# First modulation columns by TensorE, eight MLP pairs begun, folds on GpSimd: four edits to a two-layer hybrid encoder trunk

## The chip, the cores and the metric

One core of a Trainium2 chip runs the whole program in one launch. The metric is the device time of one execution in microseconds (us). The kernel before took 2339.54 us, the median of three runs (2332.86 to 2339.99). TensorE appears as PE, VectorE as DVE, ScalarE as ACT, GpSimd as POOL and SyncE, which issues the transfers, as SP.

## The reference, cut to what matters

The input is x (1, 1024, 1024) in f32, a conditioning vector c of 1024 and the weights. There are two layers. Layer 0 mixes by an mLSTM, layer 1 by multi-head latent attention. Every sub-layer is normalised before and after, and shifted, scaled and gated by rows made from c:

```python
c_act = jax.nn.silu(c)
for layer in range(DEPTH):
    sh1, sc1, g1, sh2, sc2, g2 = jnp.split(c_act @ mod_w[layer] + mod_b[layer], 6, axis=-1)
    h = modulate(rms_norm(x, norm_g[layer, 0]), sh1, sc1)
    ...
    x = x + g1[:, None, :] * rms_norm(y, norm_g[layer, 1])
    h = modulate(rms_norm(x, norm_g[layer, 2]), sh2, sc2)
    y = sq_relu_mlp(h, ffn_w1[layer], ffn_w2[layer])
    x = x + g2[:, None, :] * rms_norm(y, norm_g[layer, 3])
```

`sq_relu_mlp` is `square(relu(h @ w1)) @ w2` with w1 of 1024 x 4096. Each of the rows sh1 to g2 is a product of c_act (1024) with 1024 columns of mod_w.

## The kernel before, in words

Every large product is made of three TensorE products: both operands are cut into a high and a low part (`whi` and `wlo` of a weight, `hTh` and `hTl` or `uh` and `ul` of an activation), and `mm3` (L155 to L157) multiplies high by high, low by high and high by low. The high part is a cast on ACT, the low part a subtraction on DVE (L106, L504, L550, L754, L442), so each piece of weight passes ACT, then DVE, then PE.

The program is written in one order, and a scheduler with a timeline of its own decides for each engine in which order its instructions stand. Each engine then works through its own list in that order and waits at an instruction whose inputs are not there.

**Start.** `layer_a` normalises the first four token blocks, turns them by TensorE transposes (`turned`, L982) and multiplies them with the value weights, 344 columns at a time, for k = 0 to 7. The turned block k is shifted and scaled, for which the columns sh1 and sc1 of block k are needed. `slab(k)` loads 1024 x 256 of mod_w in two pieces, `mod_sum(k)` (L963 to L970) multiplies and adds the eight 128-row parts on DVE into two accumulators and adds these on POOL, and `mod_col` (L976) sums over partitions by two matmuls with a column of ones.

**Modulation rows.** The other rows come from `layer_mod`, through `gemv`: eight steps on DVE, each with 512 KB of mod_w (L263 for the first, L265 for seven), then eight transposes on PE (`column`, L183) with a DVE reduction. These are generators: `next(mods)` emits one step. In layer 0 two steps go with each value product (the loops below `mods`, L1045), and rows that aren't done there follow with the rest of the mixer. Three rows of layer 1 and a fourth alone (`extra`, L1732) are emitted in the up product of the MLP, one step in every third product.

**Turn to the MLP.** `mixer_out` makes the output projection block by block (n = 0 to 7), adds it to x, and calls `h_norm` (L489), which normalises a block for the MLP by itself. Blocks are turned in pairs: even and odd ones. `odd_sums` (L468, its sums are L476 to L479) makes combinations of the odd blocks with the even ones. `mlp_begin` (L625) does products 1 and 2 of the first BEGUN = 6 of 16 weight pairs, which need only the even blocks and the pair's first weights (`w_first`, L495), while the last blocks are normalised and turned, and makes the high and low parts of the combined blocks (`odd_high`, `odd_low`, L438 and L442).

**MLP.** The MLP's two products use a scheme with seven products in place of eight. In the up product (`up_product`) each pair p runs products 1, 2, 6, 7, 5, 4, 3, and the sums go to DVE (L680, L711 to L714). Weight pairs (`w_pair`) have four sums and differences on POOL (L557, L558, L570, L577), with casts and cuts on ACT (L546) and DVE (L550). In the down product (`mlp`) four token groups j accumulate y in SBUF (DVE L760 adds a PSUM bank to y), and after the last group of pairs but one, seven additions of 128 x 512 fold the accumulators (L816 to L825, all on DVE). These folds stand between DVE's splits of the next u (L754) and the adds L760 that PE waits for to get PSUM banks back; the final products follow.

Of the kernel before, what the change touches and what calls it, by code (L numbers as in the profile page):

```python
# [14 lines left out]
ALU = mybir.AluOpType  # L15
# [50 lines left out]
class Trunk:  # L66
# [356 lines left out]
    BEGUN = 6  # L423
# [65 lines left out]
    def h_norm(self, t):  # L489
        x = self.mix[5].pop(t)  # L490
        h = self.U("h")[:, :D]
        self.S.activation(h, x, AF.Copy, scale=self.rms(x, D, h))
        self.mix[6][t] = h
# [134 lines left out]
    def mlp_begin(self, l, odd):  # L628
# [8 lines left out]

        up(0, 2, 4)
        self.odd_high(0, "S2", "S3")
        self.h_norm(NT - 1)  # L640
        up(1, 3)
        self.w_step()
# [5 lines left out]
        up(3, 4, 5)  # L648
        self.odd_sums(2)
        self.w_step()  # L650
        up(4, 5)
        self.odd_high(2, "S2", "S3", "S1", "A22", "S4")
        self.odd_low(2, "S2", "S3")
        for _ in range(2):
            self.w_step()
        up(5)
        self.w_step()
        self.odd_low(2, "S1", "A22", "S4")
# [60 lines left out]
    def mlp(self, l, done, extra, last=None):  # L719
# [43 lines left out]
        for p in range(NP):  # L763
            for o, s in enumerate((1, 2, 6, 7, 5, 4, 3)):
# [6 lines left out]
                if n % 3 == 0:  # L771
                    next(extra, None)
# [13 lines left out]
        for it in range(items - 4):  # L786
# [28 lines left out]
            if g == ng - 2:  # L815
                for dst, src in (  # L816
                    (c16[:, hi], c16[:, lo]),
                    (c23[:, lo], c16[:, lo]),
                    (c47[:, hi], c16[:, hi]),
                    (c47[:, lo], c47[:, hi]),  # L820
                    (c47[:, hi], fives[j]),
                    (c16[:, hi], fives[j]),
                    (c23[:, hi], c16[:, hi]),
                ):
                    V.tensor_tensor(out=dst, in0=dst, in1=src, op=ALU.add)  # L825
                acc[j] = c23, c47
# [60 lines left out]
    def layer_a(self):  # L887
# [85 lines left out]
        def mod_col(k, acc, ps):  # L973

            for s in range(2):
                PE.matmul(ps[:, s : s + 1], acc[:, s * P : (s + 1) * P], self.ones[:, 0:1], start=True, stop=True)  # L976
# [5 lines left out]
        def turned(k):  # L982

            ps = self.MM()
            mod_col(k, sums.pop(k), ps[:, 512:])
# [16 lines left out]
        mod_sum(0)  # L1002
        for k in range(1, 4):
            slab(k)
        for k in range(1, 4):
            mod_sum(k)
# [29 lines left out]
        for tb in range(4):  # L1036
# [12 lines left out]
            + [lambda j=j: self.layer_mod(1, j) for j in (0, 1)]  # L1049
            for s in mod()  # L1050
        )
        for tb in range(4, NT):
            values(tb, proj_piece(w, tb))
            for _ in range(2):
                next(mods, None)
# [72 lines left out]
    def mixer_out(self, n, y):  # L1128
# [13 lines left out]
        if n == 5:  # L1142
            self.odd_sums(0)
        for t in {2: (0, 1), 3: (2,), 4: (3, 4), 5: (6,), 6: (5,)}.get(n, ()):
            self.h_norm(t)
# [582 lines left out]
    def run(self):  # L1728
# [3 lines left out]
        extra = [(s for j in js for s in self.layer_mod(1, j)) for js in ((2, 4, 3), (5,))]  # L1732
# [99 lines left out]
```

## Time and profile before

| | us |
|---|---|
| median of 3 runs | 2339.54 |
| lowest and highest run | 2332.86 and 2339.99 |
| the profiled execution | 2336.43 |
| its span, first to last instruction | 2334.7 |
| PE busy in it | 2208.0 (95%) |
| DVE, ACT, POOL busy | 1752.7, 1007.7, 480.7 |
| mean granted TensorE clock | 0.988 |

The profile is of one execution. In a row of the timeline stand the start, the duration, the engine, the line of the kernel, the operation, the tiles and shapes, and in brackets the idle time of that engine before the row and what ended it. A busy PE is not PE at its peak, since matmuls overlap; a pace is better read from the distance between starts.

### The profile page before, as it was taken

To read this page: it belongs to the slowest core of one execution; us is meant where nothing else is said; L and a number is where in the kernel's file an instruction comes from. 1 tells how busy PE (TensorE), PEld (TensorE's weight loads), DVE (VectorE), ACT (ScalarE), POOL (GpSimd) and SP (SyncE) were. 2 spreads that over 40 slices of the span, in tenths; PEclk is the share of its full clock that TensorE was granted. 3 is DMA by queue.
4 is the path that set the end of the run, shared out by engine and by line. 5 is a ranking of instruction groups with operands and counts; after the bars stand their busy time and mean duration, and the time that the engine had idled before them with its cause. 6 is when DMAs were issued, how large, how long until landed. Compare 5 with 4: busy or idle time off the path is not lost. (4 is left out here: it accounts for less than half of the span.)

```text
span 2334.7 us, 29139 instructions
## 1 busy us (share of the span) xinstructions
PE 2208.0 (95%) x10730; PEld 1833.8 (79%) x10730; DVE 1752.7 (75%) x2848; ACT 1007.7 (43%) x1637; POOL 480.7 (21%) x324
## 2 busy tenths in 40 slices
PE   5799999988999999999999999999889999999997
PEld 4798888866777777777798988987667888777776
DVE  6684676577888858788998676655777777588888
ACT  4421474563443464233344545544634444633321
POOL 1000110003433334231121000000034334333300
PEclk9999999999999999999999999999999999999999
DMA  9495343233665555454321000122346445544452
GB/s 272 142 322 201 100 73 99 91 109 127 221 226 189 190 180 160 119 167 146 102 88 44 17 17 15 46 73 81 109 156 220 152 149 189 172 131 140 142 174 99
DMA packets 304102, 318.09 MB, mean 136 GB/s; under 512 B 15976, under 2 KB 256216, under 8 KB 303960
## 3 DMA queue, kind: packets, MB, share of 16 engines
q1 hardware_dynamic: 303960, 316.23, 43.2%
q8 instruction: 84, 1.38, 0.2%
q14 instruction: 58, 0.48, 0.1%
HBM read 243.75 MB, written 72.43 MB: 135 GB/s over the span
## 5 line engine op out<-in xcount | busy, mean ns | idle before, releaser
L155 PE MATMUL mm<-whi,uh 128*128 128x512 f32 x688 | 273.1, 397 | 12.6 <-DVE y L760 10.7
L157 PE MATMUL mm<-whi,ul 128*128 128x512 f32 x688 | 271.2, 394 | 1.2 <-DVE ul L754 1.2
L156 PE MATMUL mm<-wlo,uh 128*128 128x512 f32 x688 | 271.1, 394 | 0.0
L577 POOL TENSOR_TENSOR tt<-raw,tt 128x512 f32<-128x512 f32 x60 | 118.0, 1967 | 668.7 <-DVE wlo L550 586.9
L760 DVE TENSOR_TENSOR y<-y,mm 128x1024 f32<-128x1024 f32 (+1 forms) x161 | 193.2, 1206 | 49.6 <-PE mm L157 49.4
L155 PE MATMUL sm<-hSh,whi 128*128 128x512 f32 x512 | 204.2, 399 | 11.3 <-DVE x L680 6.7
L157 PE MATMUL sm<-hSh,wlo 128*128 128x512 f32 x512 | 202.0, 396 | 2.2 <-DVE wlo L550 2.2
L156 PE MATMUL sm<-hSl,whi 128*128 128x512 f32 x512 | 202.5, 396 | 0.0
L550 DVE TENSOR_TENSOR wlo<-raw,whi 128x1024 fp32r<-128x1024 f32 x108 | 162.8, 1507 | 19.8 <-ACT whi L546 18.7
L754 DVE TENSOR_TENSOR ul<-u,uh 128x896 fp32r<-128x896 f32 (+1 forms) x120 | 151.0, 1289 | 32.0 <-ACT uh L748 24.4
L155 PEld LDWEIGHTS mm<-whi,uh 128*128 128x128 f32 x688 | 129.2, 188 | 49.2 <-DVE y L760 17.3
L680 DVE TENSOR_TENSOR x<-x,sm 128x512 f32<-128x512 f32 x192 | 127.8, 681 | 45.3 <-PE sm L157 41.9
L557 POOL TENSOR_TENSOR tt<-raw,raw 128x512 f32<-128x512 f32 x32 | 56.3, 1760 | 489.6 <-DVE hSl L442 461.5
L157 PEld LDWEIGHTS mm<-whi,ul 128*128 128x128 f32 x688 | 129.2, 188 | 32.4 <-DVE ul L754 2.1
L156 PEld LDWEIGHTS mm<-wlo,uh 128*128 128x128 f32 x688 | 129.2, 188 | 29.3
L748 ACT CAST uh<-u 128x896 fp32r<-128x896 f32 (+1 forms) x120 | 107.9, 945 | 84.8 <-PE mm L157 66.9
L265 DVE SCALAR_TENSOR_TENSOR acc<-modw,cact,acc 128x1024 f32<-128x1024 f32 x84 | 112.5, 1339 | 35.8 <-DMA modw<-in_mod_w_dram 29.1
L683 ACT ACTIVATE x<-x 128x1024 f32<-128x1024 f32 x64 | 67.7, 1058 | 155.2 <-DVE x L680 155.2
L582 ACT CAST w<-tt 128x512 fp32r<-128x512 f32 x60 | 37.2, 620 | 213.6 <-POOL tt L577 210.5
L155 PEld LDWEIGHTS sm<-hSh,whi 128*128 128x128 f32 x512 | 96.8, 189 | 37.9 <-DVE x L680 8.2
L546 ACT CAST whi<-raw 128x1024 fp32r<-128x1024 f32 x108 | 112.9, 1045 | 23.9 <-DVE wlo L550 10.2
L546 ACT CAST whi<-tt 128x1024 fp32r<-128x1024 f32 x60 | 62.9, 1048 | 136.9 <-issue 62.2
(404 smaller groups left out, 5991.7 us busy)
## 6 DMA issues: line engine op xcount, KB each, us to landing
raw<-in_ffn_w_dram SPq DMA_DIRECT2D x140, 512.0 KB
u<-us SPq DMA_DIRECT2D x112, 448.0 KB
us<-x SPq DMA_DIRECT2D x92, 512.0 KB
modw<-in_mod_w_dram SPq DMA_DIRECT2D x80, 512.0 KB
x<-xn SPq DMA_DIRECT2D x24, 512.0 KB
x<-x SPq DMA_DIRECT2D x24, 512.0 KB
x<-in_x_dram SPq DMA_DIRECT2D x16, 512.0 KB
slab<-in_mod_w_dram SPq DMA_DIRECT2D x32, 256.0 KB
```

The source lines that it names most:

```text
L155: mm(out, a[0], b[0], start=start, stop=False)
L156: mm(out, a[0], b[1], start=False, stop=False)
L157: mm(out, a[1], b[0], start=False, stop=stop)
L265: self.V.scalar_tensor_tensor(out=acc, in0=t, scalar=self.cact[:, k : k + 1], in1=acc, op0=ALU.mult, op1=ALU.add)
L546: S.copy(x[0], u)
L550: V.tensor_tensor(out=x[1], in0=u, in1=x[0].bitcast(F32), op=ALU.subtract)
L577: G.tensor_tensor(out=t1, in0=b21, in1=t2, op=ALU.subtract)
L680: V.tensor_tensor(out=dst, in0=src, in1=ps, op=ALU.add)
L683: S.activation(u, u, AF.Relu)
L748: S.copy(x[0], u)
L754: V.tensor_tensor(out=x[1], in0=u, in1=x[0].bitcast(F32), op=ALU.subtract)
L760: V.tensor_tensor(out=dst, in0=dst, in1=ps, op=ALU.add)
```

## The change

1. **First columns.** For k = 0 and 1 `mod_col` no longer takes a sum by DVE and POOL: 16 matmuls on PE (8 parts, 2 columns), with the slab as weights and a column of c_act as the moving operand, accumulate the two columns in PSUM. k = 2 to 7 stay as they were.
2. **Modulation rows.** The loop over the values of blocks 4 to 7 emits no steps of `mods` any more, so every row comes later; the row (1, 1) leaves `mods` and goes into `extra`, whose steps are emitted in two of five up products, in place of one of three.
3. **Begin.** BEGUN goes from 6 to 8. `h_norm` takes groups of blocks that share one reciprocal root. `odd_sums(0)` moves from block n = 5 of the output projection to the start of `mlp_begin`, whose steps are put in another order.
4. **Folds.** Four of the seven fold additions of each token group go to POOL.

```diff
-    BEGUN = 6
+    BEGUN = 8
...
-    def h_norm(self, t):
-        x = self.mix[5].pop(t)
-        h = self.U("h")[:, :D]
-        self.S.activation(h, x, AF.Copy, scale=self.rms(x, D, h))
-        self.mix[6][t] = h
+    def h_norm(self, *ts):
+        xs = [self.mix[5].pop(t) for t in ts]
+        ssq = self.W("ssqs", [P, 4])
+        hs = [self.U("h")[:, :D] for _ in ts]
+        for i, (x, h) in enumerate(zip(xs, hs)):
+            self.S.activation(h, x, AF.Square, accum_out=ssq[:, i : i + 1])
+        r = self.rsqrt(ssq[:, : len(ts)], len(ts), 1.0 / D)
+        for i, (t, x, h) in enumerate(zip(ts, xs, hs)):
+            self.S.activation(h, x, AF.Copy, scale=r[:, i : i + 1])
+            self.mix[6][t] = h
...
+        self.odd_sums(0)
         up(0, 2, 4)
+        self.h_norm(NT - 1)
         self.odd_high(0, "S2", "S3")
-        self.h_norm(NT - 1)
         up(1, 3)
-        self.w_step()
         self.odd_high(0, "S1", "A22", "S4")
         self.odd_low(0, "S2", "S3")
         up(2, 3, 5, 4)
         self.odd_turn(2, [odd.pop(5), odd.pop(7)])
         self.odd_low(0, "S1", "A22", "S4")
-        up(3, 4, 5)
+        up(3, 4, 5, 6)
         self.odd_sums(2)
+        up(4, 5, 7, 6)
+        self.odd_high(2, "S2", "S3", "S1")
         self.w_step()
-        up(4, 5)
-        self.odd_high(2, "S2", "S3", "S1", "A22", "S4")
+        up(5, 6, 7)
+        self.odd_high(2, "A22", "S4")
         self.odd_low(2, "S2", "S3")
-        for _ in range(2):
-            self.w_step()
-        up(5)
         self.w_step()
-        self.odd_low(2, "S1", "A22", "S4")
+        up(6, 7)
+        self.w_step()
+        self.odd_low(2, "S1")
+        self.w_step()
+        up(7)
+        self.w_step()
+        self.odd_low(2, "A22", "S4")
         self.w_step()
...
-                if n % 3 == 0:
+                if n % 5 in (0, 2):
                     next(extra, None)
...
-                for dst, src in (
-                    (c16[:, hi], c16[:, lo]),
-                    (c23[:, lo], c16[:, lo]),
-                    (c47[:, hi], c16[:, hi]),
-                    (c47[:, lo], c47[:, hi]),
-                    (c47[:, hi], fives[j]),
-                    (c16[:, hi], fives[j]),
-                    (c23[:, hi], c16[:, hi]),
+                for e, dst, src in (
+                    (G, c16[:, hi], c16[:, lo]),
+                    (G, c47[:, hi], c16[:, hi]),
+                    (G, c47[:, lo], c47[:, hi]),
+                    (G, c23[:, lo], c16[:, lo]),
+                    (V, c47[:, hi], fives[j]),
+                    (V, c16[:, hi], fives[j]),
+                    (V, c23[:, hi], c16[:, hi]),
                 ):
-                    V.tensor_tensor(out=dst, in0=dst, in1=src, op=ALU.add)
+                    e.tensor_tensor(out=dst, in0=dst, in1=src, op=ALU.add)
...
         def mod_col(k, acc, ps):
             for s in range(2):
-                PE.matmul(ps[:, s : s + 1], acc[:, s * P : (s + 1) * P], self.ones[:, 0:1], start=True, stop=True)
+                o = slice(s * P, (s + 1) * P)
+                if acc is not None:
+                    PE.matmul(ps[:, s : s + 1], acc[:, o], self.ones[:, 0:1], start=True, stop=True)
+                else:
+                    for i in range(KD):
+                        PE.matmul(ps[:, s : s + 1], slabs[k][i // 4][:, i % 4, o], self.cact[:, i : i + 1], start=i == 0, stop=i == KD - 1)
...
-        mod_sum(0)
         for k in range(1, 4):
             slab(k)
-        for k in range(1, 4):
+        for k in range(2, 4):
             mod_sum(k)
...
-            + [lambda j=j: self.layer_mod(1, j) for j in (0, 1)]
+            + [lambda: self.layer_mod(1, 0)]
             for s in mod()
         )
         for tb in range(4, NT):
             values(tb, proj_piece(w, tb))
-            for _ in range(2):
-                next(mods, None)
...
-        if n == 5:
-            self.odd_sums(0)
-        for t in {2: (0, 1), 3: (2,), 4: (3, 4), 5: (6,), 6: (5,)}.get(n, ()):
-            self.h_norm(t)
+        for ts in {3: ((0, 2),), 4: ((1, 3),), 5: ((4, 6),), 6: ((5,),)}.get(n, ()):
+            self.h_norm(*ts)
...
-        extra = [(s for j in js for s in self.layer_mod(1, j)) for js in ((2, 4, 3), (5,))]
+        extra = [(s for j in js for s in self.layer_mod(1, j)) for js in ((1, 2, 4, 3), (5,))]
```

Three places show what this does to the engines' lists. The names are tiles with a buffer number: `sm` and `mm` are PSUM banks, `acc` a sum of a modulation row, `ident` the matrix for transposes. Lines of the changed kernel are a few higher than those before (L504 becomes L509).

The first place is PE's list among the value products of blocks 4 to 7. Before, the first row's transposes stand here:

```order
L155 MATMUL sm_1012<-whi_552,hTh_785 128x344
L156 MATMUL sm_1012<-wlo_553,hTh_785 128x344
L157 MATMUL sm_1012<-whi_552,hTl_786 128x344
L183 MATMUL sm_1039<-ident,acc_855 128x128 x4
L183 MATMUL sm_1045<-ident,acc_855 128x128 x4
L155 MATMUL sm_1075<-whi_544,hTh_698 128x344
L156 MATMUL sm_1075<-wlo_545,hTh_698 128x344
```

In the changed kernel they stand here, and a transpose of the gates stands 55 rows behind the old place:

```order
L156 MATMUL sm_1192<-wlo_820,hTh_465 128x344
L157 MATMUL sm_1192<-whi_819,hTl_466 128x344
L183 MATMUL sm_1219<-ident,acc_1020 128x128 x4
L183 MATMUL sm_1225<-ident,acc_1020 128x128 x4
L155 MATMUL sm_1231<-whi_807,hTh_215 128x344
L156 MATMUL sm_1231<-wlo_808,hTh_215 128x344
```

The transposes went from row 392 of PE's list to row 536, 144 rows later.

The second place is the start of PE's list. `slab` is a piece of mod_w, `x` a token block. Before:

```order
L976 MATMUL mm_213<-ones,acc_151 128x1 x2
L183 MATMUL mm_213<-ident,x_95 128x128
L183 MATMUL mm_213<-ident,x_97 128x128
L183 MATMUL mm_213<-ident,x_111 128x128
L183 MATMUL mm_213<-ident,x_113 128x128
L976 MATMUL mm_252<-ones,acc_180 128x1 x2
```

After:

```order
L991 MATMUL mm_191<-cact,slab_142 128x1 x4
L991 MATMUL mm_191<-cact,slab_143 128x1 x4
L991 MATMUL mm_191<-cact,slab_142 128x1 x4
L991 MATMUL mm_191<-cact,slab_143 128x1 x4
L991 MATMUL mm_244<-cact,slab_151 128x1 x4
L991 MATMUL mm_244<-cact,slab_152 128x1 x4
L991 MATMUL mm_244<-cact,slab_151 128x1 x2
L183 MATMUL mm_191<-ident,x_95 128x128
L183 MATMUL mm_191<-ident,x_97 128x128
L183 MATMUL mm_191<-ident,x_111 128x128
L183 MATMUL mm_191<-ident,x_113 128x128
```

Sixteen matmuls of k = 0 and ten of k = 1 stand ahead of the first transposes; the other six of k = 1 and the pair of k = 2 stand behind them.

The third place is DVE's list where layer 0 turns to the MLP: `hs` and `hr` are the tiles of the odd sums, `gt` feeds the output projection, `rsy` and `rst` are steps of reciprocal roots. Before, the sums stand ahead of the last `gt`:

```order
L476 TENSOR_TENSOR hs_4253<-hr_4219,hr_4204 128x1024
L172 SCALAR_TENSOR_TENSOR rsy_4240<-rst_4241,rsy_4240 128x1
L477 TENSOR_TENSOR hs_4254<-hs_4253,hr_4037 128x1024
L478 TENSOR_TENSOR hr_4204<-hr_4037,hr_4204 128x1024
L168 SCALAR_TENSOR_TENSOR rst_4241<-rsy_4240,rsv_4239 128x1
L479 TENSOR_TENSOR hr_4052<-hr_4052,hs_4254 128x1024
L172 SCALAR_TENSOR_TENSOR rsy_4240<-rst_4241,rsy_4240 128x1
L401 SCALAR_TENSOR_TENSOR xn_4236<-mm_4155,rsy_4240,row_3548 128x1024
L402 TENSOR_TENSOR xn_4236<-xn_4236,x_4083 128x1024
L1321 TENSOR_TENSOR gt_4281<-sm_4282,sg_2407 128x512
```

After, they stand behind the splits of the first two begun pairs (L509), the last of them behind the third pair's:

```order
L509 TENSOR_TENSOR wlo_4350<-raw_4063,whi_4349 128x1024
L476 TENSOR_TENSOR hs_4440<-hr_4148,hr_4133 128x1024
L172 SCALAR_TENSOR_TENSOR rsy_4337<-rst_4338,rsy_4337 128x1
L164 TENSOR_SCALAR rsv_4406<-ssq_4404 128x1
L477 TENSOR_TENSOR hs_4441<-hs_4440,hr_3975 128x1024
L478 TENSOR_TENSOR hr_4133<-hr_3975,hr_4133 128x1024
L168 SCALAR_TENSOR_TENSOR rst_4338<-rsy_4337,rsv_4336 128x1
L165 TENSOR_SCALAR rsy_4407<-rsv_4406 128x1
L509 TENSOR_TENSOR wlo_4422<-raw_4206,whi_4421 128x1024
L479 TENSOR_TENSOR hr_3990<-hr_3990,hs_4441 128x1024
```

The four sums moved from the output projection's last blocks into the begin, around the third pair's low weights.

More of the change, by code (lines that the diff above doesn't have):

```diff
@@ L984, in turned @@
             ps = self.MM()
-            mod_col(k, sums.pop(k), ps[:, 512:])
+            mod_col(k, sums.pop(k, None), ps[:, 512:])
             self.transposes(ps, [x[:, k * P : (k + 1) * P] for x in xs[:4]])
```

## The prediction

> **What bounds the kernel now.** I read the page's busy times first, then the windows, then TensorE's rows with an idle time before them in the stages that the change touches. All times are microseconds (us) of the span.
>
> ```profile
> PE 2208.0 (95%) x10730; PEld 1833.8 (79%) x10730; DVE 1752.7 (75%) x2848; ACT 1007.7 (43%) x1637; POOL 480.7 (21%) x324
> 20.00:40.00 20.00, 13.96 (x56) 11.98 (x57) 19.29 (x50) 7.63 (x11) 5.43 (x4) 1.00 1.17 294
> 100.00:120.00 20.00, 9.53 (x55) 9.49 (x56) 17.92 (x41) 5.08 (x11) 0.00 (x0) 0.74 0.13 37
> 200.00:300.00 100.00, 100.00 (x502) 83.57 (x501) 58.48 (x99) 39.22 (x90) 9.92 (x8) 1.00 0.48 141
> 480.00:500.00 20.00, 14.44 (x59) 11.12 (x58) 10.45 (x30) 11.46 (x22) 0.00 (x0) 0.80 0.20 56
> 600.00:700.00 100.00, 96.12 (x414) 75.92 (x413) 86.36 (x96) 44.85 (x48) 43.00 (x24) 1.00 0.67 220
> 1100.00:1200.00 100.00, 95.18 (x473) 80.67 (x472) 95.76 (x242) 31.68 (x71) 14.83 (x8) 1.00 0.31 104
> 1600.00:1700.00 100.00, 86.37 (x376) 68.47 (x376) 66.84 (x139) 59.02 (x103) 6.48 (x5) 0.93 0.37 108
> ```
>
> A window row gives its length, then busy time (instructions) of PE, PEld, DVE, ACT and POOL, the granted clock, the DMA share and GB/s. PE is full at 200 to 300; nothing is to be had there. Of the span PE idles 2334.7 - 2208.0 = 127, and the change aims at the four places where the rows show idleness: the start, 100 to 120 (10.5 of 20 idle, and the clock down to 0.74), the turn from mixer to MLP (480 to 500, 1600 to 1700, again with a lower clock), and the end of a down product (DVE 95.8% busy at 1100 to 1200). PE's total work hardly changes, so every term below is idleness of PE, or half-clock time, gained or lost.
>
> **The row moved off the values.**
>
> ```profile
> 110.47 1.94 PE L183 MATMUL sm<-ident,acc 128*128 128x128 f32 x8 [10.55 <-DVE acc L265]
> 96.91 0.74 DVE L263 TENSOR_SCALAR acc<-modw,cact 128x1024 f32<-128x1024 f32 x1
> 109.05 1.27 DVE L265 SCALAR_TENSOR_TENSOR acc<-modw,cact,acc 128x1024 f32<-128x1024 f32 x1
> ```
>
> Eight transposes of the first modulation row's sum stand in PE's order ahead of value matmuls that need nothing of it, while DVE works at that sum from 96.91 to 110.32 among gates and rope tables. The value matmuls behind them start at this pace:
>
> ```profile
> 112.49 0.49 PE L156 MATMUL sm<-wlo,hTh 128*128 128x344 f32 x1
> 112.78 0.49 PE L157 MATMUL sm<-whi,hTl 128*128 128x344 f32 x1
> ...
> 113.97 0.32 PE L157 MATMUL sm<-whi,hTl 128*128 128x344 f32 x1
> 114.13 0.32 PE L155 MATMUL sm<-whi,hTh 128*128 128x344 f32 x1
> ```
>
> Now 144 rows of PE's order lie between the old place and the new one; at 0.16 apiece (113.97 to 114.13) they are 23 us, so PE, which stopped at 110.47 - 10.55 = 99.9, comes there at 123, a little later with the waits below. DVE, with the same sum plus three splits and more gate steps put ahead, should be done at about 119 to 121: an estimate from the 13.4 it took before and some 8 more of work. The 10.55 go. So does the half clock that followed until about 113.3 (starts 0.29 apart at 112.49, 0.16 at 113.97): 2.8 us at half rate, 1.4. New is that a gate transpose, which waits for DVE's gate chain, stands 55 rows behind the old place, so PE is there at 99.9 + 55 x 0.16 = 108.7. DVE has two steps of the sum, a first one and some 20 of gates and tables ahead of it from 96.91: about 109 to 110, an estimate by the same rows, so 0 to 2 of waiting. Term: -10.55 - 1.4 + 1 = **-11**, bounds -12 and -7 (the new transposes waiting 3).
>
> Behind it in DVE's queue stand the splits of the next weights, which have the same cover. The later rows of the mixer move by one place; the 200 to 300 row shows PE full there at a DMA share of 0.48, so I take 0.
>
> **The first columns on PE.**
>
> ```profile
> 31.23 1.50 PE L155 MATMUL sm<-whi,hTh 128*128 128x344 f32 x4
> 33.05 1.01 PE L976 MATMUL mm<-ones,acc 128*128 128x1 f32 x4 [0.32 <-POOL acc L970]
> 40.79 0.50 PE L976 MATMUL mm<-ones,acc 128*128 128x1 f32 x4
> 46.49 0.61 PE L976 MATMUL mm<-ones,acc 128*128 128x1 f32 x4 [1.87 <-POOL acc L970]
> 13.76 0.61 DVE L967 TENSOR_SCALAR acc<-slab,cact 128x256 f32<-128x256 f32 x2 [1.52 <-DMA slab<-in_mod_w_dram]
> 21.48 1.28 DVE L969 SCALAR_TENSOR_TENSOR acc<-slab,cact,acc 128x256 f32<-128x256 f32 x3 [0.30 <-DMA slab<-in_mod_w_dram]
> ```
>
> One matmul of a single column is two in the trace (fp32), so four rows are two of them: 0.50 apiece at the low clock (33.05), 0.25 at the full one (40.79). The 16 for k=0 start when the slab lands, 13.8, and end at 13.8 + 8 = 22; ten of the 16 for k=1 stand ahead of the first transposes and their last slab lands at 21.5: 27. Then a set of transposes (1.2), six more matmuls (3.0), a pair for k=2 (1.0) and two sets of transposes (2.3): the first value matmul at 34.5 against 31.23, so +3.3. Against it: 16 DVE steps less, 16 x 0.43 = 7 us, and DVE's sums were what the 1.87 at 46.49 waited for. Term: **+1.5**, bounds -3 and +5.
>
> The lower bound is the clock: if the columns raised it, the values between 31.23 (low) and 40.79 (full) would save at most half of that time, 4.8. The row at 33.05 still takes 1.01, although PE had been busy since 31.23 but for 0.32, so I take it that single columns don't raise it. The Trainium skill (TensorE: Matmul & The Clock Gate, Part 1) says otherwise: some 3.4 us of sustained activity bring the full clock, whatever is issued. By that rule the term would be about -2; no row here shows a long run of columns.
>
> **Eight pairs begun, sums of the odd block later, shared rsqrt.**
>
> ```profile
> 466.55 1.22 DVE L476 TENSOR_TENSOR hs<-hr,hr 128x1024 f32<-128x1024 f32 x1
> 470.21 1.22 DVE L479 TENSOR_TENSOR hr<-hr,hs 128x1024 f32<-128x1024 f32 x1
> 476.83 0.50 PE L155 MATMUL mm<-whi,aTh 128*128 128x512 f32 x1 [1.11 <-ACT aTh L105]
> 493.14 0.77 PE L155 MATMUL mm<-hSh,whi 128*128 128x512 f32 x1 [3.37 <-DVE xn L401]
> 496.52 0.79 PE L157 MATMUL mm<-hSh,wlo 128*128 128x512 f32 x1 [2.19 <-DVE wlo L504]
> 534.06 0.50 PE L157 MATMUL mm<-hSh,wlo 128*128 128x512 f32 x1 [2.06 <-DVE wlo L504]
> 556.64 0.50 PE L155 MATMUL sm<-hSh,whi 128*128 128x512 f32 x1 [2.34 <-ACT whi L546]
> 1622.40 2.82 PE L183 MATMUL sm<-ident,h 128*128 128x128 f32 x12 [2.58 <-ACT h L492]
> 1658.21 0.79 PE L157 MATMUL mm<-hSh,wlo 128*128 128x512 f32 x1 [2.67 <-DVE wlo L504]
> 1718.03 0.50 PE L155 MATMUL sm<-hSh,whi 128*128 128x512 f32 x1 [2.35 <-ACT whi L546]
> ```
>
> Four sums (L476 to L479, 4 x 1.22 = 4.9) leave DVE's queue ahead of the last output projection: the 1.11 at 476.83 goes, and 0.3 beside it. The 3.37 and the 2.19 are a chain of normalising, turning and splitting the last blocks, whose DVE order hardly changes; shared rsqrt steps take about 1 off it. But the sums come back inside the begin, ahead of the third pair's split. A begun pair's 24 products need 24 x 96.12 / 414 = 5.6 us (600 to 700), and DVE was late before.
>
> ```profile
> 503.00:541.00 38.00, 33.47 (x148) 26.10 (x147) 32.95 (x44) 23.38 (x40) 8.81 (x6) 1.00 0.48 135
> ```
>
> With 33 of 38 busy and 4.9 more put in, DVE has no room there, so I expect 1 to 2 of new idleness at the fourth pair's low half. The two added pairs bring 11 us of PE work that needs only first weights. They cover the 2.34 at 556.64 (a weight pair late from POOL) and part of the 2.06. Their four transfers of 512 KB more fall where the DMA share is 0.2 to 0.5: nothing. Sum for the first layer: -1.4 - 1 + 1.5 - 2.3 - 1 = -4; if the half clock goes too (20 x 0.20 = 4 of clock time in the window at 480, part of it while PE idles), another -3. I take **-5**, bounds -12 and +2. The second layer has the same chain with 2.58, 2.67 and 2.35; its clock lost 100 x 0.07 = 7 at 1600 to 1700, and the grouping changes which block is late: **-4**, bounds -10 and +3.
>
> The row put into the up product adds a sum's eight steps:
>
> ```profile
> L265 DVE SCALAR_TENSOR_TENSOR acc<-modw,cact,acc 128x1024 f32<-128x1024 f32 x84 | 112.5, 1339 | 35.8 <-DMA modw<-in_mod_w_dram 29.1
> ```
>
> 7 x 1.34 + 0.74 = 10 us of DVE where the 600 to 700 row has 86% busy, and 4 MB on a queue whose DMA share is 0.67. PE idles 3.9 there. **+1**, bounds 0 and +4.
>
> **Folds on POOL.**
>
> ```profile
> L825 DVE TENSOR_TENSOR y<-y x16: 677/680/694, 1091.2 to 2281.2; 128x512 f32<-128x512 f32 x16
> L577 POOL TENSOR_TENSOR tt<-raw,tt 128x512 f32<-128x512 f32 x60 | 118.0, 1967 | 668.7 <-DVE wlo L550 586.9
> L155 PE MATMUL mm<-whi,uh 128*128 128x512 f32 x69 | 27.7, 401 | 4.3 <-DVE y L760 4.2
> L760 DVE TENSOR_TENSOR y<-y,mm 128x1024 f32<-128x1024 f32 (+1 forms) x161 | 193.2, 1206 | 49.6 <-PE mm L157 49.4
> 515.58 1.63 POOL L557 TENSOR_TENSOR tt<-raw,raw 128x512 f32<-128x512 f32 x1 [173.72 <-DVE hSl L442]
> 514.16 1.28 DVE L442 TENSOR_TENSOR hSl<-hs,hSh 128x512 fp32r<-128x512 f32 x2
> 515.37 5.81 DVE L442 TENSOR_TENSOR hSl<-hr,hSh 128x512 fp32r<-128x512 f32 x4
> ```
>
> Per layer 16 folds of 0.68 leave DVE: -10.9. They take POOL about 1.97 each, and POOL is free there. But four DVE steps took 5.81 where two alone took 1.28, while three POOL steps ran from 515.58 on: (5.81 - 2.56) / 3 = 1.1 of DVE lost for each POOL step that meets DVE steps reading SBUF alone. Steps with a PSUM input don't show it: L760's mean is 1.21 over all the down products, with POOL at work in most of them. About half of DVE's time around 1100 is of the first kind, so 16 x 1.1 / 2 = 9 comes back: -2 net. PE's idleness there behind L760 is 4.2 (the group of 1080 to 1145, whose first row is the third of this fence); I take **-1** for both layers, bounds -5 and +6 (all sixteen meeting: 17.6 - 10.9).
>
> **Sum.** -11 + 1.5 - 5 - 4 + 1 - 1 = -18.5. Against the profiled execution, 2336.4 (span 2334.7), that is 2317.9; it lies 3.1 below the median of three, 2339.5, from which it would be 2321. I say **2320**.
>
> **Rivals.**
> Only the values gain (chance 0.20): the begin's idleness forms again, since DVE is the late one there and gets the sums back. 2339.5 - 11 + 1.5 and the rest nothing: 2330. The 0.80 and 0.93 windows would stay.
> The half clock goes as well (0.15): the low clock at 480 and at 1600 vanishes, -3 each beyond the sum, and the start comes to -2 (-3.5): 2310.
> POOL's folds hold up DVE (0.07), the one that ends slower: if each fold blocks DVE for all its 1.97, the layer at 1100 pays 16 x 1.97 - 10.9 = 20.6 where DVE is 95.8% busy, the other perhaps half: 2339.5 + 31 - 17.5 (the other terms) = 2353. Slower than before begins where the 24 folds' worth cost more than the 17.5, at 0.68 + 17.5 / 24 = 1.4 of DVE apiece. The 1.1 measured speaks against, a busy queue behind L760 for. The Trainium skill has this rule (SBUF — State Buffer, Who interferes with whom): a DVE step with two SBUF inputs and a GpSimd step that reads SBUF lock each other out for a whole instruction.
> No change (0.10): the start at +5, the begin at its upper bounds (+5) and the folds at +2 eat the 11: 2339.
> The forecast has 0.48.
>
> A run can tell about 0.3%, 7 us, from nothing. Faster: 0.48 + 0.15 + 0.20 less a little of the 2330 case that falls within 7: 0.81. Same 0.12, slower 0.07. The range takes in the first two rivals and the bounds of the start and the begin: 2306 to 2334.
>
> **What would show it.** Right: no idleness of 10 before the row transposes, which now stand near 123 to 128, and a clock near 1 at 100 to 120; 1 to 4 more us before the first value matmul; no idleness of 2 behind weight pairs after the begin; DVE near 1100 less busy. Wrong: those transposes waiting on DVE again at their new place, or L754 and L1398 at twice their time near 1100 while POOL folds, with PE's idleness behind L760 above 5.

## The result: slower, and the profile after

The changed kernel takes 2364.94 us (median of four runs, 2361.78 to 2369.52) against 2339.76 for the kernel before: a ratio of 1.0113 with a 95% interval of 1.0082 to 1.0144. It is 25 us slower where 2320 had been forecast, outside the range.

The page of the changed kernel has these spans and busy times, first line and part 1:

```profile
span 2359.8 us, 29225 instructions
PE 2228.4 (94%) x10786; PEld 1850.3 (78%) x10786; DVE 1743.7 (74%) x2770; ACT 1007.5 (43%) x1637; POOL 523.8 (22%) x354
```

DVE has less to do than before (1752.7), POOL 43 us more, as the edits said; TensorE idles 131 in place of 127 and is busy for 20 us more. Some 7 of the 20 are the added matmuls of the first columns (up to the last transposes of x it is busy 36.1 in place of 28.9, and idles 8.9 less). Some 10 are the clock, an estimate: 2359.8 x 0.016 = 38 us of it were not granted, where before it was 2334.7 x 0.012 = 28. Behind a new wait matmuls start 0.43 apart for a while and not 0.23 (from 455.01 on, for one), so a wait costs more than its own length. The windows that answer to those of before:

```profile
20.00:40.00 20.00, 17.54 (x92) 17.36 (x92) 16.55 (x43) 6.36 (x10) 4.01 (x3) 1.00 1.15 296
100.00:120.00 20.00, 17.27 (x88) 15.58 (x87) 19.15 (x38) 9.93 (x17) 0.00 (x0) 0.91 0.57 184
460.00:480.00 20.00, 15.44 (x70) 12.54 (x69) 8.05 (x25) 11.10 (x19) 0.00 (x0) 0.83 0.25 79
600.00:700.00 100.00, 93.67 (x404) 74.45 (x403) 92.43 (x101) 45.13 (x48) 47.76 (x28) 1.00 0.75 242
1100.00:1200.00 100.00, 92.60 (x443) 76.95 (x443) 90.41 (x190) 29.81 (x60) 34.70 (x21) 0.98 0.32 104
1640.00:1660.00 20.00, 10.98 (x54) 8.80 (x53) 6.13 (x20) 10.43 (x19) 0.00 (x0) 0.82 0.19 61
```

The hole at 100 to 120 is closed (17.3 busy in place of 9.5, clock 0.91 in place of 0.74). But there is a hole now that was not there, at 460 to 480 (18.45 busy at a clock of 1.00 before), and a deeper one at 1640 to 1660 (16.07 at 0.84 before), and the up and down products (600, 1100) are a little emptier.

The same events in the two timelines (first or last TensorE row of a kind) cut the program into stages:

| stage, by TensorE's rows | before | after | change |
|---|---|---|---|
| start to the last transposes of x | 55.2 | 53.6 | -1.5 |
| to the last projection of q, k and o | 329.2 | 320.7 | -8.5 |
| to the first begun product, layer 0 (output projection) | 108.7 | 117.2 | +8.5 |
| begin and up product, to the first down product | 343.0 | 351.6 | +8.6 |
| down product and latent, to the first latent value product | 404.0 | 408.7 | +4.7 |
| to the end of attention | 310.1 | 312.1 | +2.0 |
| to the first begun product, layer 1 (output projection) | 104.6 | 112.1 | +7.5 |
| begin and up product, to its last product | 337.3 | 337.6 | +0.3 |
| down product, to its last product | 331.6 | 335.2 | +3.6 |

So 10 us came where they were expected, and 35 went elsewhere. A difference of 1 or 2 in a stage of one profile can be the clock alone: up to the last transposes of x it was 0.97 before and 1.00 after, which is the 1.5 there. The rows of TensorE with the largest new waits in the changed kernel, two in each output projection, then the begin, the up product and the first down product:

```profile
453.43 0.47 PE L155 MATMUL mm<-whi,aTh 128*128 128x512 f32 x1 [2.99 <-DVE rst L170]
473.57 0.79 PE L155 MATMUL mm<-whi,aTh 128*128 128x512 f32 x1 [4.56 <-ACT aTh L105]
525.17 0.50 PE L155 MATMUL mm<-hSh,whi 128*128 128x512 f32 x1 [2.87 <-ACT x L697]
695.50 0.50 PE L155 MATMUL sm<-hSh,whi 128*128 128x512 f32 x1 [3.67 <-DVE x L690]
1124.55 0.50 PE L155 MATMUL mm<-whi,uh 128*128 128x512 f32 x1 [2.09 <-DVE y L770]
1133.32 0.50 PE L155 MATMUL mm<-w,uh 128*128 128x512 f32 x1 [2.49 <-DVE y L770]
1635.13 0.47 PE L155 MATMUL mm<-whi,oTh 128*128 128x512 f32 x1 [2.43 <-DVE rsv L164]
1658.99 0.79 PE L155 MATMUL mm<-whi,oTh 128*128 128x512 f32 x1 [9.02 <-ACT oTh L105]
```

Around the wait of 4.56, ACT (with one row of TensorE) and DVE of the changed kernel look like this:

```profile
461.79 1.91 PE L183 MATMUL sm<-ident,h 128*128 128x128 f32 x16
462.65 2.84 ACT L457 ACTIVATE hr<-sm,modcol 128x256 f32<-128x256 f32 x6 [4.97 <-PE sm L183]
465.36 1.05 ACT L178 ACTIVATE xn<-mm 128x1024 f32<-128x1024 f32 x1
...
470.91 1.06 ACT L494 ACTIVATE h<-xn 128x1024 f32<-128x1024 f32 x1 [2.47 <-DVE xn L402]
471.96 1.03 ACT L507 CAST whi<-raw 128x1024 fp32r<-128x1024 f32 x1
472.90 1.13 ACT L105 CAST aTh<-gt 128x512 fp32r<-128x512 f32 x2
```

```profile
466.52 0.15 DVE L164 TENSOR_SCALAR rsv<-ssq 128x1 f32<-128x1 f32 x1 [11.13 <-ACT xn L178]
468.33 1.28 DVE L401 SCALAR_TENSOR_TENSOR xn<-mm,rsy,row 128x1024 f32<-128x1024 f32 x1
469.65 1.23 DVE L402 TENSOR_TENSOR xn<-xn,x 128x1024 f32<-128x1024 f32 x1
470.79 1.28 DVE L1331 TENSOR_TENSOR gt<-sm,sg 128x512 f32<-128x512 f32 x2
```

The cast `aTh` feeds the next block's projection. On DVE its source `gt` stands behind the residual (L401, L402) of a block that TensorE has finished, and on ACT the cast itself stands behind that block's square for the MLP (L494). That order is not new; the kernel before has it too, and TensorE waits 1.11 there (476.83):

```profile
460.28 2.19 PE L183 MATMUL sm<-ident,h 128*128 128x128 f32 x16
464.42 1.04 ACT L178 ACTIVATE xn<-mm 128x1024 f32<-128x1024 f32 x1
474.18 1.06 ACT L178 ACTIVATE h<-xn 128x1024 f32<-128x1024 f32 x1 [6.68 <-DVE xn L402]
476.17 1.14 ACT L105 CAST aTh<-gt 128x512 fp32r<-128x512 f32 x2
```

New is when the residual begins. Its first step (L178 on `xn`) stands on ACT behind the copies of the turned blocks (`hr`), and these wait for the transposes of the normalised blocks. Before, the transposes stand between two projections: the one ends at 460.4, the next starts at 462.2. Now they stand inside a projection, 8.4 behind its start at 453.43. So L178 begins 15 after its block left TensorE (450.4 to 465.36) in place of 4 (460.4 to 464.42). The residual, `gt` and `aTh` follow as late, and TensorE runs out of work.

### The profile page after: what moved, and what is told of

Read it like the earlier page. It is cut to its first block, busy times and chain, and to the rows that moved or that the text cites. A ratio compares the mean times of both kernels' runs of the same rounds, so it can differ in the third digit from the quotient of the medians.

```text
span 2359.8 us, 29225 instructions
## 1 busy us (share of the span) xinstructions
PE 2228.4 (94%) x10786; PEld 1850.3 (78%) x10786; DVE 1743.7 (74%) x2770; ACT 1007.5 (43%) x1637; POOL 523.8 (22%) x354
## 5 line engine op out<-in xcount | busy, mean ns | idle before, releaser
L770 DVE TENSOR_TENSOR y<-y,mm 128x1024 f32<-128x1024 f32 (+1 forms) x161 | 193.5, 1206 | 57.0 <-PE mm L157 56.6
L555 DVE TENSOR_TENSOR wlo<-raw,whi 128x1024 fp32r<-128x1024 f32 x104 | 154.1, 1482 | 15.4 <-ACT whi L551 15.3
L155 PE MATMUL mm<-hSh,whi 128*128 128x512 f32 x256 | 107.0, 418 | 22.0 <-ACT x L697 13.3
L265 DVE SCALAR_TENSOR_TENSOR acc<-modw,cact,acc 128x1024 f32<-128x1024 f32 x84 | 120.5, 1435 | 2.3 <-DMA modw<-in_mod_w_dram 0.8
```

Source lines behind the costliest of these rows:

```text
L155: mm(out, a[0], b[0], start=start, stop=False)
L265: self.V.scalar_tensor_tensor(out=acc, in0=t, scalar=self.cact[:, k : k + 1], in1=acc, op0=ALU.mult, op1=ALU.add)
L555: V.tensor_tensor(out=x[1], in0=u, in1=x[0].bitcast(F32), op=ALU.subtract)
L770: V.tensor_tensor(out=dst, in0=dst, in1=ps, op=ALU.add)
```

## The experiments

Fifteen kernels. The first eight ask which edits lose, by undoing one at a time or doing one alone; times are medians, ratios are against the kernel before with their 95% intervals.

**Folds back on DVE, in the changed kernel.**

```diff
-                for e, dst, src in (
-                    (G, c16[:, hi], c16[:, lo]),
...
+                for dst, src in (
+                    (c16[:, hi], c16[:, lo]),
```

> The changed kernel with all seven folds of each token group on DVE again, in their old order. First theory (POOL's folds and DVE's splits L764 lock each other out, so that L770 comes late and TensorE waits): the down products lose 4.8 and 2.4 us less, and the kernel takes about 2365 - 7 = 2358. Rival (the down product is late for other reasons, such as the weights or the mixed products that follow): within 2 of 2365, and the idleness before L770 near 1100 to 1135 stays above 5.

2360.87 (1.0096, 1.0072 to 1.0120): 4 less than the changed kernel, in the direction of the first theory and short of its size; the two intervals overlap, so this run alone doesn't decide.

**Norms one by one, in the changed kernel.**

```diff
-        for ts in {3: ((0, 2),), 4: ((1, 3),), 5: ((4, 6),), 6: ((5,),)}.get(n, ()):
-            self.h_norm(*ts)
+        for t in {2: (0, 1), 3: (2,), 4: (3, 4), 5: (6,), 6: (5,)}.get(n, ()):
+            self.h_norm(t)
```

> The changed kernel with each block normalised by itself again, at its old place in the output projection; the odd sums stay at the start of the begin. First theory (the squares of a group stand ahead of the casts that the output projection waits for): the idleness of 3.0 and 4.6 in layer 0 and of 2.4 and 9.0 in layer 1 goes, and the kernel takes 2365 - 8 - 7 = about 2350. Rival (the odd sums and the eight pairs, put elsewhere in the program, changed the scheduler's order there): the idleness stays, and the time is within 4 of 2365.

2345.54 (1.0038, 1.0026 to 1.0049): 19 less than the changed kernel, about what the first theory said and 5 more. No wait of 1.5 or more is left in layer 0's output projection before the first begun product; in layer 1's one of 2.65 is, which the kernel before has too (2.58). The transposes stand between the projections again, and in layer 0 L178 begins 4 after its block left TensorE, as before. So the groups are the cause, as the first theory said; that casts stand behind squares, its reason, is so in the kernel before as well.

**The row (1, 1) back in the mixer.**

```diff
-            + [lambda: self.layer_mod(1, 0)]
+            + [lambda j=j: self.layer_mod(1, j) for j in (0, 1)]
...
-                if n % 5 in (0, 2):
+                if n % 3 == 0:
```

> The changed kernel with the row (1, 1) back among the rows of the mixer, and one step of the other rows in every third up product as before; the loop over the values still emits none. First theory (eight more steps of 1.3 to 1.4 us on a DVE that is over 90% busy hold up L690, and TensorE waits): the up product of layer 0 gets about 6 us shorter, its idleness behind L690 falls from some 12 to about 5, and the kernel takes about 2359. Rival (the up product's idleness comes from the eight pairs and their weights): 2363 to 2367, with the idleness of 600 to 800 unchanged.

2380.30 (1.0181, 1.0161 to 1.0202): 15 slower than the changed kernel. Both theories are wrong: the moved row and its spacing are not a loss but the one gain.

**The old begin, in the changed kernel.**

```diff
-    BEGUN = 8
+    BEGUN = 6
...
+        if n == 5:
+            self.odd_sums(0)
...
-        self.odd_sums(0)
         up(0, 2, 4)
         self.odd_high(0, "S2", "S3")
```

> The changed kernel with six pairs begun, the old order of the begin and the odd sums after block n = 5 again; the groups of blocks that share a reciprocal root stay. First theory (grouping alone makes the output projection wait, and eight pairs give nothing): the idleness in the output projections stays or grows, and the time is 2365 within 5. Rival (the rearranged begin is what hurt): the output projections run through as before, and the kernel takes 2350 or less.

2356.01 (1.0075, 1.0056 to 1.0094): 9 less, between the two theories. The output projections wait more than before (8.8 and 11.8 at their worst rows), so the begin is not their cause; and the up product of layer 1 takes 327 where the changed kernel takes 338 and the one before 337. That pointed to the spacing of the rows' steps, which this kernel shares with the changed one.

**The values alone, in the kernel before.**

```diff
             values(tb, proj_piece(w, tb))
-            for _ in range(2):
-                next(mods, None)
```

> The kernel before, with one edit of the change alone: the loop over the values of blocks 4 to 7 emits no modulation steps. First theory (TensorE waits 10.55 us there for a sum that nothing near it needs): 2340 - 11 = 2329, with no idleness of more than 3 between 95 and 130. Rival (the steps not emitted there come back as waits in the rest of the mixer, which now has all eight rows to take): 2336 to 2344.

2335.66 (0.9992, 0.9979 to 1.0005): nothing. The 10.55 are gone, with 2.71 in their place, but all eight rows now come in the rest of the mixer, and one wait comes back there:

```profile
279.40 0.80 PE L155 MATMUL mm<-hTh,whi 128*128 128x512 f32 x1 [3.56 <-ACT sg L1103]
```

By the end of the projections of q, k and o the lead is 0.5, where the changed kernel, with seven rows, has 10.1 and no wait there. The rival holds. The same wait stands in both other kernels with eight rows in the mixer and no steps in the values (3.54 in "the row (1, 1) back", 3.55 in "three undone"), and in none with seven.

**The first columns alone.** (The edit is the one of the change in `mod_col`, `turned` and the first `mod_sum` calls.)

> The kernel before, with the first two modulation columns by TensorE alone. First theory (26 single-column matmuls ahead of the first transposes cost what the lighter DVE gives back): the last value product of the first half starts within 2 us of before, and the time is 2340 within 4. Rival (the columns raise the clock early or free DVE for more): 3 to 5 us faster, 2335 to 2337.

2342.15 (1.0027, 1.0013 to 1.0042): a loss of 5 or 6 against the runs beside it. The first theory's "same" is at its edge; the rival fell. In the profile it is 1.1 behind at the last transposes of x and 6.0 at the end of attention. The later 5 are not waits: in the two profiles TensorE idles 118.8 in place of 126.6. The clock is lower, 0.985 in the median of these seven runs and 0.988 in that of the eighteen of the kernel before; 0.003 x 2337 = 7 us is an estimate of what that costs. Why it is lower isn't shown.

**The folds alone.** (The edit is that of the change.)

> The kernel before, with four of seven folds on POOL alone. First theory (POOL's folds hold up DVE's splits): 2340 + 7 = 2347, L754 in threes at 5 us and more beside the folds. Rival (folds on POOL free DVE, and the loss in the changed kernel came from its other edits): 2335 to 2340.

2344.39 (1.0036, 1.0022 to 1.0049): 7 slower, as the first theory said. DVE has beside POOL's folds

```profile
1097.73 5.42 DVE L754 TENSOR_TENSOR ul<-u,uh 128x896 fp32r<-128x896 f32 x3
1103.08 1.21 DVE L760 TENSOR_TENSOR y<-y,mm 128x1024 f32<-128x1024 f32 x1
```

where the kernel before has two such splits in 2.08

```profile
1096.05 2.08 DVE L754 TENSOR_TENSOR ul<-u,uh 128x896 fp32r<-128x896 f32 x2
```

and TensorE waits for that L760 and its followers, over the whole kernel 21.6 behind L760 in place of 14.7:

```profile
1104.34 0.50 PE L155 MATMUL mm<-w,uh 128*128 128x512 f32 x1 [1.61 <-DVE y L760]
1118.12 0.50 PE L155 MATMUL mm<-whi,uh 128*128 128x512 f32 x1 [1.58 <-DVE y L760]
1126.88 0.50 PE L155 MATMUL mm<-w,uh 128*128 128x512 f32 x1 [2.47 <-DVE y L760]
1131.72 0.47 PE L155 MATMUL mm<-whi,uh 128*128 128x512 f32 x1 [1.80 <-DVE y L760]
```

**Three undone together.** (The edits of the first three experiments in one kernel.)

> The changed kernel with grouping, folds on POOL and the moved row (1, 1) undone together; the first columns, the values without modulation steps, the later odd sums and the eight pairs stay. First theory (these three make the loss, and the losses add): 2365 - 15 - 7 - 6 = 2337, or less where the eight pairs give something: 2325 to 2337. Rival (the loss is in the begin): above 2345.

2353.47 (1.0078, 1.0058 to 1.0097): above 2345, the rival's case, and far from the sum of the first theory. With the norms undone (2345.54) a further undoing of folds and row makes it 8 slower. So the edits had to be sorted anew: rows good, begin bad.

**All of the second edit, alone.**

```diff
-            + [lambda j=j: self.layer_mod(1, j) for j in (0, 1)]
+            + [lambda: self.layer_mod(1, 0)]
...
             values(tb, proj_piece(w, tb))
-            for _ in range(2):
-                next(mods, None)
...
-                if n % 3 == 0:
+                if n % 5 in (0, 2):
...
-        extra = [... for js in ((2, 4, 3), (5,))]
+        extra = [... for js in ((1, 2, 4, 3), (5,))]
```

> The kernel before with all of the second edit and nothing else: no modulation steps in the loop over the values, the row (1, 1) in the up product, its steps in two of five products. Theory after eight runs (the values gain about 10 only when the mixer has one row less to take; two of five costs layer 0 some 3 and gives layer 1's up product 10): 2338 - 10 + 3 - 10 = 2321. Rival (the row costs the up product what the values give, as in the changed kernel): 2334 to 2340.

2319.83 (0.9922, 0.9907 to 0.9938): 18 faster than before, as the theory said, and the fastest kernel of the study. In its profile the lead is 12.2 at the end of the projections of q, k and o and 20.3 at the end; layer 0's begin and up product keep their length (342.5 against 343.0), layer 1's lose 7.

**The new begin alone.** (The edits of BEGUN and `mlp_begin`; `odd_sums(0)` moves with it, the norms stay single.)

> The kernel before with eight pairs begun, the begin in its new order and the odd sums at its start, each block still normalised by itself. Theory after eight runs (eight pairs cost each layer 6 to 13 of new waits for PSUM banks and weights, while the odd sums put later give each output projection 3 to 4): 2338 + 2 x 10 - 7 = about 2351. Rival (the eight pairs only look bad together with other edits): 2330 to 2340.

2356.38 (1.0076, 1.0061 to 1.0092): 19 slower, as the theory said and 5 more. The output projections win 3 and 6, the begins with the up products lose 13 and 12. Of these, 7.4 and 6.6 are idle time of TensorE; the rest goes with the clock, 0.97 there in place of 0.98.

**The rows with the odd sums late.**

```diff
-        if n == 5:
-            self.odd_sums(0)
...
+        self.odd_sums(0)
         up(0, 2, 4)
```

> The rows kernel of this call with the odd sums moved to the start of the begin, six pairs begun in the old order. Theory (the output projections lose 3 to 4 of waiting each, the begin has room for 4.9 of sums only in part): 2321 - 7 + 4 = 2318. Rival (the sums come back in full as waits in the begin): 2321 to 2326.

2323.01 (0.9935, 0.9922 to 0.9947): within the noise of the rows alone or 3 worse, the rival's case. Layer 0's begin and up product take 350.4 in place of 342.5. A wait of 2.88 behind ACT (L688, the copy out of a fresh PSUM bank) has come back about 35 into it. It stands in layer 0 of all seven kernels that have the odd sums in the begin (2.87 or 2.88), and in none of the others.

**The spacing alone.**

```diff
-                if n % 3 == 0:
+                if n % 5 in (0, 2):
```

> The kernel before with one line changed: the rows of layer 1 emit their steps in two of five up products in place of one of three. Theory (the spacing alone moves the scheduler's order so that layer 1's up product runs through, 10 less): 2328 to 2331. Rival (the 10 came from the other edits): 2335 to 2341.

2323.33 (0.9944, 0.9925 to 0.9963): one line, 13 or 14 faster, some 5 more than the theory said. Layer 1 from its begin through its up product, the kernel before and then this one:

```profile
1655.00:1992.00 337.00, 321.35 (x1366) 255.71 (x1366) 257.18 (x304) 156.77 (x186) 124.90 (x71) 0.98 0.51 165
```

```profile
1651.00:1979.00 328.00, 319.18 (x1365) 255.67 (x1366) 260.58 (x304) 156.35 (x186) 119.30 (x71) 0.99 0.53 169
```

The same work, 9 less: TensorE's idle time goes from 15.7 to 8.8, and it is busy 2.2 less, at a clock of 0.99 in place of 0.98. The waits of 2.35 (ACT whi), 1.53, 0.93, 1.14 and 0.98 of the kernel before are gone.

**The rows with eight pairs, odd sums at their old place.** (BEGUN 8 and the new order of `mlp_begin` without its first line, on top of the rows.)

> The rows kernel (no modulation steps in the values, row (1, 1) in the up product, two steps in five) with eight pairs begun in the new order, the odd sums left after block n = 5. Theory (the eight pairs themselves lose time: fresh PSUM banks wait behind ACT's casts): 2320 + 8 to 16 = 2328 to 2336. Rival (the odd sums inside the begin were the whole loss of the new begin, the eight pairs with their spare work give some back): 2314 to 2322.

2329.71 (0.9966, 0.9953 to 0.9979): 10 worse than the rows alone, as the theory said, but not for its reason. The first 78 us of layer 0's MLP, this kernel and then the rows alone, hold the same work:

```profile
482.00:560.00 78.00, 69.99 (x288) 54.72 (x289) 55.37 (x85) 39.87 (x61) 17.94 (x11) 0.93 0.38 111
```

```profile
480.00:558.00 78.00, 70.56 (x296) 55.58 (x297) 64.21 (x95) 41.62 (x62) 19.68 (x12) 0.96 0.48 142
```

The loss comes later in the up product: waits of 3.6 twice and 2.0 twice between 200 and 300 us into it, and 9.5 us in layer 0 against 1.3 in layer 1. Of the 9.5, 4.9 are idle time; the rest goes with the clock (0.97 in that stage in place of 0.99). A fresh PSUM bank stands behind one of the waits of 2.0 alone, so the banks are not the main cause; and a wait of 3.73 stands 176 us into that stage with the new spacing and nothing else, so not all of it is of the eight pairs.

**The other two of five.**

```diff
-                if n % 3 == 0:
+                if n % 5 in (1, 3):
```

> The kernel before with the rows of layer 1 emitting steps in two of five up products, but the first and third of five in place of the second and fifth. Theory one (the place counts: the first and third products of a begun pair are those with DVE's longest work behind them): at least half of the 14 gained by the other spacing is lost, 2330 to 2340. Theory two (only the number of steps per product counts, or any order but one of three): 2321 to 2327.

2333.67 (0.9981, 0.9972 to 0.9991): 10 of the 14 are lost again, so for the whole kernel the place of the steps counts more than their number. By layers it is mixed: layer 1's begin and up product keep 6.0 of the 9.3 that they had won (331.3 against 337.3 before), and layer 0's take 347.1, where they took 341.2 with the other spacing and 343.0 before. The largest new wait is in layer 1, where a row's reduction comes before the up product's adds:

```profile
1774.13 0.76 PE L155 MATMUL sm<-hSh,w 128*128 128x512 f32 x1 [3.50 <-DVE modcol L274]
```

**The grouping alone.** (The edits of `h_norm` and of its calls in `mixer_out`.)

> The kernel before with the blocks normalised in groups that share a reciprocal root, alone. Theory (grouping is what makes the output projections wait): 2337 + 15 to 20 = 2352 to 2357, with waits of 3 and more in both output projections. Rival (grouping hurts only together with the late odd sums): 2337 to 2344.

2354.03 (1.0074, 1.0058 to 1.0089): 17 slower, and the two waits in each output projection stand there without any other edit:

```profile
464.23 0.77 PE L155 MATMUL mm<-whi,aTh 128*128 128x512 f32 x1 [2.94 <-DVE rst L170]
487.63 0.79 PE L155 MATMUL mm<-whi,aTh 128*128 128x512 f32 x1 [8.11 <-ACT aTh L105]
1631.75 0.47 PE L155 MATMUL mm<-whi,oTh 128*128 128x512 f32 x1 [2.43 <-DVE rsv L164]
1656.87 0.80 PE L155 MATMUL mm<-whi,oTh 128*128 128x512 f32 x1 [11.86 <-ACT oTh L105]
```

Each part alone, as a share of the kernel before (2337 in those runs):

| part alone | ratio | us |
|---|---|---|
| rows: values, (1, 1), spacing | 0.9922 | -18 |
| new begin with the odd sums | 1.0076 | +18 |
| grouped norms | 1.0074 | +17 |
| folds on POOL | 1.0036 | +8 |
| first columns | 1.0027 | +6 |
| sum | | +31 |
| the whole change | 1.0113 | +26 |

The parts add up to the whole within about 5, which is less than their intervals leave open (3 to 4 us to each side for a part, 7 for the whole).

## Why the prediction was wrong, point by point

**The values: the size about right, a condition missed.** The waits went as forecast in the changed kernel (10.55 became 2.73 at the gate transposes; the row's transposes stand at 127.37 and don't wait), and that stage is 8.5 shorter, where I had 11. But I put 0 to "the later rows of the mixer move by one place". With eight rows that is worth nearly all of the gain (0.9992 for the values alone): the lead lasts only because a row left the mixer in the same change.

```profile
108.45 0.18 PE L1204 MATMUL sm<-ident,gate 32*1 32x32 f32 x1 [2.73 <-DVE gate L1195]
127.37 1.04 PE L183 MATMUL sm<-ident,acc 128*128 128x128 f32 x8
```

**The first columns: about the size at the start, for other reasons, and a loss elsewhere.** I had +1.5, with +5 as the upper bound; alone they cost 5 to 6. At the start the first value product came 1.4 late, not 3.3, as the columns fill time in which TensorE had waited (it idles 17.5 up to the last transposes of x, in place of 26.4), and the 1.87 at 46.49 that was to go stayed at 1.86. In these rows of the changed kernel the columns run one after the other from 14.70 to 24, at 5.49 / 25 = 0.22 each, and the pair at 27.57 still takes 1.01:

```profile
14.70 5.49 PE L991 MATMUL mm<-cact,slab 128*128 128x1 f32 x25 [0.80 <-DMA slab<-in_mod_w_dram]
27.57 1.01 PE L988 MATMUL mm<-ones,acc 128*128 128x1 f32 x4
46.51 0.61 PE L988 MATMUL mm<-ones,acc 128*128 128x1 f32 x4 [1.86 <-POOL acc L980]
```

That is the low pace throughout, so the columns themselves ran 9 us without bringing the full one, as I had read from the row of before (33.05). The rule of the Trainium skill (TensorE: Matmul & The Clock Gate, Part 1), some 3.4 us of activity, doesn't hold for this stretch. But I was wrong to take it that the columns leave the clock as it is: behind them the value products start 0.16 apart from 35.02 on, 2.4 after the first of them, and in the kernel before 0.29 apart up to 38.09, 6.9 after the first. The full clock begins at 33.8 to 35.6 in the seven kernels with the columns and at 35.9 to 39.3 in the ten without. The gain doesn't last: over the whole kernel the clock is lower with the columns alone, for a cause that is open.

**The begin: the step that failed.** I wrote that the chain of the last blocks is one "whose DVE order hardly changes; shared rsqrt steps take about 1 off it". I counted the instructions that a group saves and looked at the order at the begin. I did not look at the order in the output projection, where ACT's and TensorE's lists change: a group is normalised as one, its transposes stand inside the next projection and not ahead of it, ACT's copies of them hold up the residual of the block just finished, and the casts for the next block stand behind that residual. Grouping alone costs 17, and its profile shows the same: transposes at 471.63, 7.4 into a projection that starts at 464.23, and L178 14 after its block left TensorE. The edit also moves some calls of `h_norm` (blocks 0, 1 and 4 are normalised one or two steps later); no run separates the shared root from the later calls.

The two added pairs were to bring cover, and the wait of 2.34 behind the first weight pair did go from the changed kernel. That was luck: with the eight pairs alone it stands in both layers (2.34 and 2.35), and with the new spacing of the rows alone it is gone. The eight pairs cost 10 beside the rows, and the odd sums in the begin bring a wait of 2.87, behind a copy on ACT, where I had 1 to 2 at the fourth pair's low half. In the sum I had -9 for all this; measured alone, new begin and grouping are +35.

**The moved row: about right, with a gain left out.** The row itself costs layer 0's begin and up product 1.3 (342.5 with it, 341.2 without, both at the new spacing; TensorE's idle time there is 18.0 against 14.8, so it can be 3), where I had +1 with +4 as the upper bound. That all steps go to other products has no term in my sum: alone it is worth 14.

**The folds: the sign wrong, the mechanism known.** I had -1 for both layers, with +6 as the upper bound, which counts the sixteen folds of one layer only; alone they cost 7 to 8. In the changed kernel three splits beside POOL's folds take 5.42:

```profile
1101.56 1.08 DVE L764 TENSOR_TENSOR ul<-u,uh 128x896 fp32r<-128x896 f32 x1
...
1103.70 5.42 DVE L764 TENSOR_TENSOR ul<-u,uh 128x896 fp32r<-128x896 f32 x3
1109.03 1.21 DVE L770 TENSOR_TENSOR y<-y,mm 128x1024 f32<-128x1024 f32 x1
```

```profile
1101.72 4.20 POOL L835 TENSOR_TENSOR y<-y,y 128x512 f32<-128x512 f32 x2 [3.29 <-DVE y L770]
1106.00 2.03 POOL L835 TENSOR_TENSOR y<-y 128x512 f32<-128x512 f32 x1
```

One by one, the three splits took 1.08, 2.17 and 2.32. The second ends 0.95 after the fold that ran from 1103.92 to 1105.92, the third 1.08 after the one from 1106.00 to 1108.03: as if each did its work once the fold beside it was over. So the two folds cost DVE 2.2, 1.1 each, which is the 1.1 of my working, against the 0.68 that leaves DVE with each. DVE's sum came out about as I had it, too: with the folds alone it is busy 1746.7 in the whole kernel, 6 less than before, where I had -2 a layer. The step that failed is the next one, that TensorE's wait follows DVE's busy time: it rose from 14.7 to 21.6 behind L760 while DVE had less to do. I had taken the loss as an average; it falls where the split and the fold both become ready, just after an add, and ahead of an L770 that TensorE waits for. The Trainium skill (SBUF — State Buffer, Who interferes with whom) has the rule that I had given the slower rival, that the two lock each other out for a whole instruction. The trace agrees: a split pays what is left of the fold, and not the 1.97 of a whole one that the rival took.

**The rivals.** None of them is what happened. The slower one had 0.07 and was one of four causes; I had no rival in which an edit hurts a stage that it isn't meant for.

What stays open: why the place of a row's steps among the products is worth up to 14, beyond that five named waits go; how eight pairs cost layer 0 waits 200 us later; and why the first columns lower the clock. The first two act through the order that the scheduler writes, and no run here fixes that order and changes one thing.

## What to carry to other kernels

Where engines work through fixed lists, price an edit by what now stands ahead of whatever the busiest engine waits for next, in every stage the edited lines reach, and not by the instructions it saves. A wait that is removed stays removed only if the work moved out of its way has a place to go; test that by the stage's end, not by the wait. Take an edit of several parts apart before judging it: here one part alone (0.9922) beats both kernels, and its smallest line (0.9944) makes most of that.

## What the runs showed of the hardware that was not expected

A run of 44 single-column fp32 matmuls from 14.70 on stayed at 0.22 us each, and the pair at 27.57 at the 1.01 that goes with the low pace (0.50 at the full one, at 40.79 of the kernel before). The four splits of 128x896 that met a running fold of POOL in the changed kernel (two in each layer) took 2.17 to 2.32 and ended 0.95 to 1.08 after that fold, where a split alone takes 1.08. DVE's adds with a PSUM input stayed at 1.21, also the 49 of 161 beside POOL (in the kernel before 42 of 161, and not most of them, as my working says).
